# Half-size first loads with VectorE sums, and two mid weights made by an accumulating DMA, in a causal convolution kernel

## The chip, the cores and the metric

The kernel runs on one core of a Trainium2 chip (trn2). The time is device microseconds of one execution. Before the change it is 783.65 us (median of 6 runs, 783.41 to 783.91, beside the runs of the changed kernel). A profile is one further execution, seen by the hardware profiler; its span is about 2 us shorter than the time. PE is TensorE, DVE is VectorE, ACT is ScalarE, POOL is GpSimd, SP is SyncE.

All runs quoted are of one state (fast). A ratio is the mean time of one kernel's fast runs over that of the other's of the same rounds, so it isn't quite the ratio of the medians that are quoted beside it.

## The reference

```python
B, S, D, K = 8, 4096, 512, 8
for k in range(K):
    shifted = x if k == 0 else np.concatenate(
        [np.zeros((B, k, D), np.float32), x[:, :-k, :]], axis=1)
    out += np.matmul(shifted, kernel[k])
```

Eight taps, each a 512x512 matrix. The error allowed is that of bf16 inputs with f32 sums.

## The kernel before: the parts that matter

The kernel computes the taps with a three-level Karatsuba-like scheme. For that it needs sums of rows of the transposed input and differences of taps. A tap lies in `W[a, b, c]` with each index LO or HI; an index MID means a difference, so `W[MID, HI, HI] = W[HI, HI, HI] - W[LO, HI, HI]`. There are 19 such mid weights.

The input is split into 128 runs of 256 rows, one run a partition; block i holds 8 rows of each run, in two halves h. I write x00, x01, x10, x11, x20 ... for block i, half h. Each half is loaded by GpSimd (f32 to bf16 in the DMA), then transposed to `XT`. x00, x01 and x10 are transposed by PE through PSUM; from x11 on a DMA issued by SyncE does it. `H` is the history: the last rows of the neighbouring run.

```python
def load(out, src):
    nc.gpsimd.dma_start(out=out, in_=src)

def transpose_x(i, h):                       # from x11 on
    nc.sync.dma_start_transpose(out=XT[:, 4 * h:4 * h + 4, :]..., in_=xin[i, h]...)

def mid_dve(*which):                         # all 19 mid weights
    o, u, v = mid(*which)
    tt(o, u, v, SUB)

def sums_pe(name, k, *sums):                 # row sums of x00 and the history, on PE
    ...
    for n, t in enumerate(ts_):
        src, idt = (xin[0, 0][:, t], ident) if t >= 0 else (H[:, 8 + t], identh)
        nc.tensor.matmul(pw[:, h, c * P:(c + 1) * P], lhsT=src[:, c * P:(c + 1) * P],
                         rhs=idt, start=n == 0, stop=n == len(ts_) - 1, ...)

load(H[1:P, 4:8], xr[0:P - 1, RUN - 4:RUN, :])
load_x(0, 0)
# ... later, in GpSimd's order:
# load_w(4), history, load_w(6), load_w(5), load_w(7), load_x(0, 1), load_x(1, 0),
# load_w(0), load_w(2), load_w(1), load_w(3), load_x(1, 1), load_x(2, 1), load_x(2, 0)
```

Node 0 is built from 16 plain products (`direct`, 4 matmuls each); the other 95 nodes have 9 products. A node's PSUM sum often starts from a value that ScalarE writes there (`node_seed`), on which the matmuls then add.

Of the kernel before, what the change touches and what calls it, by code (L numbers as in the profile page):

```python
# [22 lines left out]
def kernel(  # L23
# [6 lines left out]
    nc = tc.nc  # L30
# [53 lines left out]
    def load_x(i, h):  # L84
        xin[i, h] = xpool.tile([P, 4, D], bf, name="xin")
        load(xin[i, h], xr[:, K * i + 4 * h:K * i + 4 * h + 4, :])
# [45 lines left out]

# [6 lines left out]
    load(H[1:P, 4:8], xr[0:P - 1, RUN - 4:RUN, :])  # L139
    load_x(0, 0)  # L140
    ident = spool.tile([P, P], bf, name="ident")
    make_identity(nc, ident)

    identh = spool.tile([P, P], bf, name="identh")
    nc.gpsimd.tensor_copy(out=identh, in_=ident)
    nc.gpsimd.memset(identh[:, 0:P:G], 0.0)
    identn = spool.tile([P, P], bf, name="identn")
    nc.gpsimd.tensor_scalar_mul(out=identn, in0=ident, scalar1=-1.0)  # L148
# [20 lines left out]

    bank = {}  # L170

    def mid_pe(h, k, *which):
        o, u, v = mid(*which)
        bank[which, h] = pair(k)
        for c in range(2):
            pw = bank[which, h][:, c]
            nc.tensor.matmul(pw, lhsT=ident, rhs=u[:, 2 * h + c], start=True, stop=False)
            nc.tensor.matmul(pw, lhsT=identn, rhs=v[:, 2 * h + c], start=False, stop=True)

    def mid_act(h, *which):  # L180
        nc.scalar.copy(out=mid(*which)[0][:, 2 * h:2 * h + 2], in_=bank[which, h])
# [13 lines left out]

    def sums_pe(name, k, *sums):

        pw = bank[name] = pair(k)
        for h, ts_ in enumerate(sums):
            for c in range(DC):  # L200
                for n, t in enumerate(ts_):
                    src, idt = (xin[0, 0][:, t], ident) if t >= 0 else (H[:, 8 + t], identh)
                    nc.tensor.matmul(pw[:, h, c * P:(c + 1) * P], lhsT=src[:, c * P:(c + 1) * P],
                                     rhs=idt, start=n == 0, stop=n == len(ts_) - 1,
                                     skip_group_check=True)
# [141 lines left out]





    load_w(4)
    transpose_pe("xh", 2, H, 5, 8)
    sums_pe("d4a", 1, (-4, 0), (-3, 1))
    load(H[1:P, 1:4], xr[0:P - 1, RUN - 7:RUN - 4, :])
    load_w(6)
    sums_pe("d4b", 2, (-2, 2), (-1, 3))
    nc.vector.tensor_copy(out=XF[:, 0:3], in_=bank["xh"])  # L358
    transpose_pe("xf", 2, xin[0, 0], 0, 4)
    load_w(5)  # L360
    nc.vector.tensor_copy(out=D4[:, 0:2], in_=bank["d4a"])
    nc.scalar.copy(out=D4[:, 2:4], in_=bank["d4b"])
    n0.p = {0: pair(0), 1: pair(1)}
    fill(pair(3))
    load_w(7)
    direct(0, 2)
    direct(0, 1)
    direct(0, 3)
    nc.scalar.copy(out=XF[:, 3:7], in_=bank["xf"])  # L369
    sums_pe("e4a", 2, (-5, -1), (-6, -2))  # L370
    nc.vector.memset(XF[:, 0:3, 0:D:G], 0.0)
    tt(D2, XF[:, 0:5], XF[:, 2:7], ADD)
    direct(2, 3)
    tt(F21, D2[:, 0:4], D2[:, 1:5], ADD)
    mid_dve(1, LO, HI)
    sums_pe("e4b", 2, (-7, -3))
    direct(1, 2)
    direct(0, 0)
    load_x(0, 1)
    tt(D1, XF[:, 2:4], XF[:, 3:5], ADD)  # L380
    mid_dve(2, LO, HI)
    nc.scalar.copy(out=E4[:, 3:1:-1], in_=bank["e4a"])
    mid_dve(2, LO, LO)
    load_x(1, 0)
    load_w(0)
    nc.vector.tensor_copy(out=E4[:, 1], in_=bank["e4b"][:, 0])
    direct(1, 3)
    direct(1, 1)
    transpose_pe("x1", 2, xin[0, 1], 0, 4)
    nc.scalar.copy(out=XT[:, 4:8], in_=bank["x1"])  # L390
# [60 lines left out]
    load_x(2, 0)
# [201 lines left out]
```

## Time and profile before

| | before |
|---|---|
| time, median | 783.65 us |
| span of the profile | 780.9 us |
| PE busy | 767.4 us, 98% |
| x01, x10, x11 landed | 25.0, 27.5, 40.1 us |
| transposing DMA of x11: issued, to landing | 40.20 us, 4.9 us |
| PE's wait behind x11 | 0.74 us, at 48 us |

Read it from the end of the chain backwards: the span is PE's work plus what PE doesn't get to do at the start. So only PE's waits before 98 us are to be had. The prediction below shows the lines.

### The profile page before, as it was taken

To read this page: it belongs to the slowest core of one execution; us is meant where nothing else is said; L and a number is where in the kernel's file an instruction comes from. 1 tells how busy PE (TensorE), PEld (TensorE's weight loads), DVE (VectorE), ACT (ScalarE), POOL (GpSimd) and SP (SyncE) were. 2 spreads that over 40 slices of the span, in tenths; PEclk is the share of its full clock that TensorE was granted. 3 is DMA by queue.
4 is the path that set the end of the run, shared out by engine and by line. 5 is a ranking of instruction groups with operands and counts; after the bars stand their busy time and mean duration, and the time that the engine had idled before them with its cause. 6 is when DMAs were issued, how large, how long until landed. Compare 5 with 4: busy or idle time off the path is not lost.

```text
span 780.9 us, 9507 instructions
## 1 busy us (share of the span) xinstructions
PE 767.4 (98%) x3620; PEld 349.0 (45%) x3620; DVE 659.3 (84%) x764; ACT 283.2 (36%) x460; POOL 42.8 (5%) x83
## 2 busy tenths in 40 slices
PE   7899999999999999999999999999999999999997
PEld 4444444444444444444444444444444444444443
DVE  4899888888888889888898888898888898888895
ACT  2453433333333333343324343333343333343332
POOL 5000000000000000000000000000000000000000
PEclk9999999999999999999999999999999999999999
DMA  9963979778788777878777788877787877788753
GB/s 163 210 120 114 237 176 207 169 187 167 178 179 206 174 176 173 177 184 194 184 171 168 179 190 188 191 166 179 165 187 187 195 170 182 166 172 200 179 153 123
DMA packets 159229, 138.37 MB, mean 177 GB/s; under 512 B 130130, under 2 KB 134226, under 8 KB 159184
## 3 DMA queue, kind: packets, MB, share of 16 engines
q1 hardware_dynamic: 145312, 98.84, 46.3%
q0 software_dynamic: 13728, 38.66, 31.1%
q8 instruction: 28, 0.46, 0.2%
q10 hardware_dynamic: 144, 0.26, 0.1%
q14 instruction: 17, 0.14, 0.1%
HBM read 77.32 MB, written 67.11 MB: 185 GB/s over the span
## 4 chain that ended last, share of the span: by engine, by line
PE 94%; DMA 3%; DVE 1%; POOL 1%; issue 0%; ACT 0%; DVEq 0%; POOLq 0%
PE pp L215 94%; DMA xin<-in_x_dram 2%; DMA XT<-xin 1%; POOL w L80 0%; DVE D L76 0%; PE pp L192 0%; DVE pp L76 0%; ACT XT L390 0%; DVE y L76 0%; POOL D L80 0%; DVEq L648 0%; POOL xin L80 0%; POOL identn L148 0%; PE pp L186 0%; POOL ident masks.py:199 0%
## 5 line engine op out<-in xcount | busy, mean ns | idle before, releaser
L215 PE MATMUL pp<-w,D 128*128 128x512 bf16 x3280 | 715.8, 379 | 1.7 <-DMA w<-in_kernel_dram 0.9
L215 PEld LDWEIGHTS <-D 128*128 128x128 bf16 x3280 | 320.2, 98 | 390.4 <-issue 2.8
L76 DVE TENSOR_TENSOR D<-D 128x2048 bf16<-128x2048 bf16 (+2 forms) x250 | 227.2, 948 | 3.4 <-ACT D L369 3.4
L76 DVE TENSOR_TENSOR y<-pp,ms 128x1024 f32<-128x1024 f32 (+1 forms) x121 | 146.4, 1212 | 45.3 <-PE pp L215 45.3
L76 DVE TENSOR_TENSOR D<-XT 128x2048 bf16<-128x2048 bf16 (+2 forms) x153 | 142.5, 947 | 12.1 <-DMA XT<-xin 10.4
L262 ACT COPY pp<-pp 128x512 f32<-128x512 f32 x95 | 54.1, 570 | 260.6 <-PE pp L215 260.6
L274 ACT COPY pp<-pp 128x512 f32<-128x512 f32 x95 | 54.2, 570 | 167.1 <-PE pp L215 165.6
L76 DVE TENSOR_TENSOR pp<-dts,pp 128x512 f32<-128x512 f32 x95 | 65.7, 691 | 43.9 <-ACT dts L280 42.6
L317 ACT COPY ms<-pp 128x1024 f32<-128x1024 f32 x60 | 61.0, 1016 | 35.0 <-PE pp L215 33.0
L80 POOL DMA_DIRECT2D xin<-in_x_dram x64 | 34.0, 531 | 692.5 <-DMA XT<-xin 675.8
L290 DVE SCALAR_TENSOR_TENSOR pp<-pp,dts 128x512 f32<-128x512 f32 x95 | 66.0, 695 | 3.2
L280 ACT COPY dts<-pp 128x512 f32<-128x512 f32 x95 | 57.5, 606 | 0.0
L276 ACT ACTIVATE pp<-pp 128x512 f32<-128x512 f32 x95 | 56.1, 590 | 0.8 <-PE pp L215 0.8
L215 PE MATMUL pp<-w,XT 128*128 128x512 bf16 x120 | 30.8, 379 | 0.0
L76 DVE TENSOR_TENSOR w<-w,w 128x2048 bf16<-128x2048 bf16 x19 | 22.9, 1219 | 1.5 <-DMA w<-in_kernel_dram 1.3
L215 PEld LDWEIGHTS <-XT 128*128 128x128 bf16 x120 | 11.7, 98 | 14.2
L186 PE MATMUL pp<-zero,ident 128*128 128x512 bf16 x20 | 6.7, 493 | 3.1 <-POOL ident masks.py:199 3.1
L215 PE MATMUL pp<-w,F 128*128 128x512 bf16 x36 | 8.7, 379 | 0.2 <-DVE pp L76 0.2
L215 PE MATMUL pp<-w,w 128*128 128x512 bf16 x36 | 8.3, 379 | 0.0
L192 PE MATMUL pp<-ident,xin 128*128 128x128 bf16 x48 | 3.2, 219 | 3.6 <-DMA xin<-in_x_dram 1.4
L80 POOL DMA_DIRECT2D w<-in_kernel_dram x8 | 6.1, 785 | 0.5 <-DMA w<-in_kernel_dram 0.5
L358 DVE COPY D<-pp 128x1536 bf16<-128x1536 bf16 x1 | 1.0, 958 | 6.1 <-PE pp L192 6.1
(59 smaller groups left out, 78.7 us busy)
## 6 DMA issues: line engine op xcount, KB each, us to landing
out_dram<-y SPq DMA_DIRECT2D x123, 512.0 KB, 3.4
xin<-in_x_dram POOLq DMA_DIRECT2D x64, 512.0 KB, 6.0
w<-in_kernel_dram POOLq DMA_DIRECT2D x8, 512.0 KB, 15.7
out_dram<-ms SPq DMA_DIRECT2D x2, 512.0 KB, 5.4
out_dram<-f SPq DMA_DIRECT2D x2, 512.0 KB, 6.3
XT<-xin SPq DMA_TRANSPOSE x61, 6.1
D<-in_x_dram POOLq DMA_DIRECT2D x1, 508.0 KB, 5.6
D<-in_x_dram POOLq DMA_DIRECT2D x1, 381.0 KB, 9.4
```

The lines of the kernel that those rows point to most:

```text
L76: nc.vector.tensor_tensor(out=o, in0=a, in1=b, op=op)
L80: nc.gpsimd.dma_start(out=out, in_=src)
L186: nc.tensor.matmul(pw[:, h], lhsT=ident, rhs=zero, start=True, stop=True)
L192: nc.tensor.transpose(o[:, t - t0, c * P:(c + 1) * P], src[:, t, c * P:(c + 1) * P], ident)
L215: nc.tensor.matmul(bank, lhsT=comp[:, c * P:(c + 1) * P], rhs=w[:, c, :], start=start and c == 0, stop=c == DC - 1, skip_group_check=True)
L262: nc.scalar.copy(out=n.q[:, 0], in_=n.q[:, 1])
L274: nc.scalar.copy(out=n.p[b_][:, 1], in_=n.q[:, 1])
L276: nc.scalar.mul(out=n.p[b_][:, 1], in_=n.q[:, 1], mul=-1.0)
L280: nc.scalar.copy(out=n.dts, in_=n.q[:, 0])
L290: nc.vector.scalar_tensor_tensor(out=p[:, 0], in0=p[:, 1], scalar=-1.0, in1=n.dts, op0=MUL, op1=SUB)
L317: nc.scalar.copy(out=ms[b_], in_=p)
L358: nc.vector.tensor_copy(out=XF[:, 0:3], in_=bank["xh"])
```

## The change

Its intent is to start node 0 earlier (first loads in halves, row sums by VectorE instead of PE) and to relieve VectorE of two mid weights (ScalarE writes the negated LO weight, a DMA adds the HI weight to it in SBUF). The order of nearly everything in the first 100 us moves too; most of that is cut here. `load_h(a, b)` loads a part of the history, `load_x(0, 0, 0, 2)` the first two rows of x00. `XF` holds transposed rows of the history and of x00, `D4` their sums.

```diff
+    load_h(-4, -2)
+    load_x(0, 0, 0, 2)
-    load(H[1:P, 4:8], xr[0:P - 1, RUN - 4:RUN, :])
-    load_x(0, 0)
...
+    def mid_neg(u, v):
+        nc.scalar.mul(out=W[MID, u, v], in_=W[LO, u, v], mul=-1.0)
+
+    def mid_acc(u, v):
+        nc.gpsimd.dma_start(out=W[MID, u, v], in_=W[HI, u, v], accum_op=ADD)
...
-    def sums_pe(name, k, *sums):
...
+    transpose_pe("x0", 2, xin[0, 0], 0, 2)
+    nc.vector.tensor_copy(out=XF[:, 4:6], in_=bank["x0"])
+    nc.vector.tensor_copy(out=XF[:, 0:2], in_=bank["h0"])
+    tt(D4[:, 0:2], XF[:, 0:2], XF[:, 4:6], ADD)
...
+    load_x(1, 1)
+    mid_acc(HI, HI)
+    mid_acc(LO, HI)
...
+    load_x(2, 0)
...
+    load_x(2, 1)
...
-    mid_dve(0, HI, HI)
...
-    mid_dve(0, LO, HI)
```

More of the change, by code (lines that the diff above doesn't have):

```diff
@@ L82, with load_x @@
     xin = {}
-    def load_x(i, h):
-        xin[i, h] = xpool.tile([P, 4, D], bf, name="xin")
-        load(xin[i, h], xr[:, K * i + 4 * h:K * i + 4 * h + 4, :])
+    def load_x(i, h, a=0, b=4):
+        if a == 0:
+            xin[i, h] = xpool.tile([P, 4, D], bf, name="xin")
+        t0 = K * i + 4 * h
+        load(xin[i, h][:, a:b], xr[:, t0 + a:t0 + b, :])
     def transpose_x(i, h):
@@ L138, with load_h @@
     H = D421
-    load(H[1:P, 4:8], xr[0:P - 1, RUN - 4:RUN, :])
-    load_x(0, 0)
+    def load_h(a, b):
+        load(H[1:P, 8 + a:8 + b], xr[0:P - 1, RUN + a:RUN + b, :])
+    load_h(-4, -2)
+    load_x(0, 0, 0, 2)
     ident = spool.tile([P, P], bf, name="ident")
     make_identity(nc, ident)
-    identh = spool.tile([P, P], bf, name="identh")
-    nc.gpsimd.tensor_copy(out=identh, in_=ident)
-    nc.gpsimd.memset(identh[:, 0:P:G], 0.0)
-    identn = spool.tile([P, P], bf, name="identn")
-    nc.gpsimd.tensor_scalar_mul(out=identn, in0=ident, scalar1=-1.0)
     zero = spool.tile([P, D], bf, name="zero")
@@ L168, in mid_dve @@
         tt(o, u, v, SUB)
+    def mid_neg(u, v):
+        nc.scalar.mul(out=W[MID, u, v], in_=W[LO, u, v], mul=-1.0)
+    def mid_acc(u, v):
+        nc.gpsimd.dma_start(out=W[MID, u, v], in_=W[HI, u, v], accum_op=ADD)
     bank = {}
-    def mid_pe(h, k, *which):
-        o, u, v = mid(*which)
-        bank[which, h] = pair(k)
-        for c in range(2):
-            pw = bank[which, h][:, c]
-            nc.tensor.matmul(pw, lhsT=ident, rhs=u[:, 2 * h + c], start=True, stop=False)
-            nc.tensor.matmul(pw, lhsT=identn, rhs=v[:, 2 * h + c], start=False, stop=True)
-    def mid_act(h, *which):
-        nc.scalar.copy(out=mid(*which)[0][:, 2 * h:2 * h + 2], in_=bank[which, h])
     def fill(pw):
@@ L194, in transpose_pe @@
         bank[name] = o[:, 0:t1 - t0]
-    def sums_pe(name, k, *sums):
-        pw = bank[name] = pair(k)
-        for h, ts_ in enumerate(sums):
-            for c in range(DC):
-                for n, t in enumerate(ts_):
-                    src, idt = (xin[0, 0][:, t], ident) if t >= 0 else (H[:, 8 + t], identh)
-                    nc.tensor.matmul(pw[:, h, c * P:(c + 1) * P], lhsT=src[:, c * P:(c + 1) * P],
-                                     rhs=idt, start=n == 0, stop=n == len(ts_) - 1,
-                                     skip_group_check=True)
     for r in range(2):
@@ L346, with first_run @@
     C0, C1 = W[MID, HI, MID], W[MID, LO, MID]
-    load_w(4)
-    transpose_pe("xh", 2, H, 5, 8)
-    sums_pe("d4a", 1, (-4, 0), (-3, 1))
-    load(H[1:P, 1:4], xr[0:P - 1, RUN - 7:RUN - 4, :])
+    def first_run(z):
+        nc.vector.memset(z[:, :, 0:D:G], 0.0)
+    transpose_pe("h0", 0, H, 4, 6)
+    load_h(-2, 0)
+    load_x(0, 0, 2, 4)
+    load_w(4)
+    transpose_pe("x0", 2, xin[0, 0], 0, 2)
+    nc.vector.tensor_copy(out=XF[:, 4:6], in_=bank["x0"])
+    nc.vector.tensor_copy(out=XF[:, 0:2], in_=bank["h0"])
@@ L356 @@
+    first_run(XF[:, 0:2])
+    tt(D4[:, 0:2], XF[:, 0:2], XF[:, 4:6], ADD)
+    transpose_pe("xb", 2, xin[0, 0], 2, 4)
+    n0.p = {0: pair(0), 1: pair(1)}
+    transpose_pe("h1", 0, H, 6, 8)
+    nc.scalar.copy(out=XF[:, 6:8], in_=bank["xb"])
+    nc.scalar.copy(out=XF[:, 2:4], in_=bank["h1"])
+    direct(0, 0)
+    load_h(-7, -4)
+    first_run(XF[:, 2:4])
     load_w(6)
-    sums_pe("d4b", 2, (-2, 2), (-1, 3))
-    nc.vector.tensor_copy(out=XF[:, 0:3], in_=bank["xh"])
-    transpose_pe("xf", 2, xin[0, 0], 0, 4)
+    transpose_pe("he", 2, H, 1, 4)
@@ L360 @@
     load_w(5)
-    nc.vector.tensor_copy(out=D4[:, 0:2], in_=bank["d4a"])
-    nc.scalar.copy(out=D4[:, 2:4], in_=bank["d4b"])
-    n0.p = {0: pair(0), 1: pair(1)}
+    tt(D4[:, 2:4], XF[:, 2:4], XF[:, 6:8], ADD)
+    direct(0, 3)
+    direct(0, 1)
+    nc.scalar.copy(out=F0, in_=XF[:, 4])
     fill(pair(3))
-    load_w(7)
-    direct(0, 2)
-    direct(0, 1)
-    direct(0, 3)
-    nc.scalar.copy(out=XF[:, 3:7], in_=bank["xf"])
-    sums_pe("e4a", 2, (-5, -1), (-6, -2))
-    nc.vector.memset(XF[:, 0:3, 0:D:G], 0.0)
@@ L372 @@
-    tt(D2, XF[:, 0:5], XF[:, 2:7], ADD)
-    direct(2, 3)
-    tt(F21, D2[:, 0:4], D2[:, 1:5], ADD)
-    mid_dve(1, LO, HI)
-    sums_pe("e4b", 2, (-7, -3))
-    direct(1, 2)
-    direct(0, 0)
-    load_x(0, 1)
-    tt(D1, XF[:, 2:4], XF[:, 3:5], ADD)
-    mid_dve(2, LO, HI)
-    nc.scalar.copy(out=E4[:, 3:1:-1], in_=bank["e4a"])
-    mid_dve(2, LO, LO)
-    load_x(1, 0)
-    load_w(0)
-    nc.vector.tensor_copy(out=E4[:, 1], in_=bank["e4b"][:, 0])
-    direct(1, 3)
-    direct(1, 1)
-    transpose_pe("x1", 2, xin[0, 1], 0, 4)
@@ L390 @@
-    nc.scalar.copy(out=XT[:, 4:8], in_=bank["x1"])
-    load_w(2)
-    mid_dve(1, LO, LO)
-    direct(1, 0)
-    transpose_pe("x2", 2, xin[1, 0], 0, 4)
-    mid_dve(2, LO, MID)
-    load_w(1)
-    tt(D4[:, 4:8], XF[:, 3:7], XT[:, 4:8], ADD)
-    direct(2, 1)
-    nc.vector.tensor_copy(out=XT[:, 2:4], in_=bank["x2"][:, 2:4])
+    direct(0, 2)
+    direct(2, 2)
+    tt(E4[:, 1:4], bank["he"], XF[:, 1:4], ADD)
+    first_run(E4[:, 1:4])
+    tt(D2, XF[:, 1:6], XF[:, 3:8], ADD)
+    load_w(7)
+    direct(1, 0)
@@ new lines @@
+    direct(1, 3)
+    load_x(0, 1)
+    tt(D1, XF[:, 3:5], XF[:, 4:6], ADD)
+    direct(1, 2)
+    mid_dve(1, LO, HI)
+    load_x(1, 0)
+    direct(1, 1)
+    mid_dve(2, LO, HI)
+    tt(F21, D2[:, 0:4], D2[:, 1:5], ADD)
+    load_w(0)
+    mid_dve(1, LO, LO)
+    mid_dve(2, LO, LO)
+    direct(2, 3)
+    mid_dve(2, LO, MID)
+    mid_neg(HI, HI)
+    mid_neg(LO, HI)
+    transpose_pe("x1", 2, xin[0, 1], 0, 4)
+    nc.vector.tensor_copy(out=XT[:, 4:8], in_=bank["x1"])
+    tt(D4[:, 4:8], XF[:, 4:8], XT[:, 4:8], ADD)
@@ L400 @@
+    direct(2, 0)
+    nc.scalar.copy(out=C0[:, 0:2], in_=XT[:, 6:8])
+    prep_d41(HI)
+    transpose_pe("x2", 2, xin[1, 0], 0, 4)
+    nc.scalar.copy(out=XT[:, 2:4], in_=bank["x2"][:, 2:4])
+    load_w(2)
+    direct(3, 0)
     prep_d42(HI)
     nc.scalar.copy(out=XT[:, 0:2], in_=bank["x2"][:, 0:2])
-    nc.scalar.copy(out=C0[:, 0:2], in_=XT[:, 6:8])
+    direct(3, 3)
     tt(T4, XT[:, 4:8], XT[:, 0:4], ADD)
     direct(3, 1)
-    prep_d41(HI)
-    tt(T42[:, 0:2], D4[:, 6:8], T4[:, 0:2], ADD)
@@ L407 @@
-    direct(3, 0)
-    nc.scalar.copy(out=C1, in_=XT[:, 0:4])
-    direct(2, 0)
-    nc.scalar.copy(out=F0, in_=XF[:, 3])
-    direct(3, 3)
-    fill(pair(2))
-    tt(D41[:, 1], T4[:, 0], T4[:, 1], ADD)
-    load_w(3)
-    tt(T42[:, 2:4], T4[:, 0:2], T4[:, 2:4], ADD)
-    node_a1(1)
-    direct(2, 2)
+    fill(pair(2))
+    load_w(3)
+    nc.scalar.copy(out=C1, in_=XT[:, 0:4])
+    direct(3, 2)
+    tt(D41[:, 1], T4[:, 0], T4[:, 1], ADD)
+    node_a1(1)
+    tt(D41[:, 0], D4[:, 7], T4[:, 0], ADD)
@@ L418 @@
+    direct(2, 1)
+    load_w(1)
+    node_a0(nodes[1])
+    tt(T42[:, 0:2], D4[:, 6:8], T4[:, 0:2], ADD)
+    tt(T42[:, 2:4], T4[:, 0:2], T4[:, 2:4], ADD)
+    node_u(nodes[1])
+    load_x(1, 1)
+    mid_acc(HI, HI)
+    mid_acc(LO, HI)
+    tt(D421[:, 0], D42[:, 7], T42[:, 0], ADD)
     node_e(nodes[0], 0)
-    tt(D41[:, 0], D4[:, 7], T4[:, 0], ADD)
-    node_a0(nodes[1])
-    node_u(nodes[1])
-    direct(3, 2)
+    node_seed(nodes[1], 0)
     mid_dve(1, HI, HI)
-    node_seed(nodes[1], 0)
     prep_d27()
+    node_v(nodes[1], 0)
@@ L426 @@
+    mid_dve(2, HI, LO)
+    tt(D421[:, 1:4], T42[:, 0:3], T42[:, 1:4], ADD)
+    node_seed(nodes[1], 1)
     node_dts(nodes[1])
-    node_seed(nodes[1], 1)
     tt(D42[:, 3], D4[:, 1], D4[:, 3], ADD)
-    node_v(nodes[1], 0)
-    tt(D421[:, 0], D42[:, 7], T42[:, 0], ADD)
-    load_x(1, 1)
-    node_v(nodes[1], 1)
-    tt(D421[:, 1:4], T42[:, 0:3], T42[:, 1:4], ADD)
-    node_a1(2)
-    mid_dve(2, HI, LO)
-    transpose_x(1, 1)
-    mid_dve(1, HI, LO)
-    node_d(nodes[1], 0)
-    node_l(nodes[1], 0, LO)
@@ L440 @@
-    mid_dve(2, HI, MID)
-    nc.scalar.copy(out=D4[:, 2:4], in_=T4[:, 2:4])
-    node_d(nodes[1], 1)
-    load_x(2, 1)
-    node_e(nodes[0], 1)
-    node_u(nodes[2])
-    node_l(nodes[1], 0, HI)
-    node_e(nodes[1], 0)
-    node_a0(nodes[2])
-    node_seed(nodes[2], 0)
-    prep_d421(HI)
-    load_x(2, 0)
-    mid_dve(2, HI, HI)
-    node_l(nodes[1], 1, LO)
-    node_l(nodes[1], 1, HI)
-    nc.scalar.copy(out=U1, in_=XT[:, 0])
+    load_x(2, 0)
+    node_d(nodes[1], 0)
+    mid_dve(1, HI, LO)
@@ new lines @@
+    mid_dve(2, HI, HI)
+    node_a1(2)
+    node_l(nodes[1], 0, HI)
+    node_v(nodes[1], 1)
+    load_x(2, 1)
+    node_d(nodes[1], 1)
+    mid_dve(2, HI, MID)
+    prep_d421(HI)
+    node_l(nodes[1], 0, LO)
+    node_a0(nodes[2])
+    node_l(nodes[1], 1, HI)
+    node_e(nodes[1], 0)
+    node_e(nodes[0], 1)
+    nc.scalar.copy(out=D4[:, 2:4], in_=T4[:, 2:4])
+    node_u(nodes[2])
+    node_seed(nodes[2], 0)
+    node_seed(nodes[2], 1)
+    node_l(nodes[1], 1, LO)
+    node_dts(nodes[2])
+    transpose_x(1, 1)
@@ L456 @@
+    nc.scalar.copy(out=D42[:, 3], in_=T42[:, 3])
     node_v(nodes[2], 0)
+    node_v(nodes[2], 1)
     prep_d4(HI)
-    nc.scalar.copy(out=D42[:, 3], in_=T42[:, 3])
-    node_seed(nodes[2], 1)
-    node_v(nodes[2], 1)
-    node_dts(nodes[2])
-    mid_dve(0, HI, HI)
-    node_e(nodes[1], 1)
     prep_d41(HI)
     node_d(nodes[2], 0)
-    node_l(nodes[2], 0, HI)
-    tt(A1[:, 0], C0[:, 1], C1[:, 0], ADD)
-    prep_d42(HI)
-    node_d(nodes[2], 1)
-    transpose_x(2, 0)
-    mid_dve(0, LO, HI)
     node_a1(3)
@@ L473 @@
     node_l(nodes[2], 0, LO)
+    mid_dve(0, LO, LO)
+    mid_dve(0, HI, LO)
+    prep_d42(HI)
+    node_l(nodes[2], 0, HI)
     node_a0(nodes[3])
+    node_d(nodes[2], 1)
+    node_u(nodes[3])
     node_e(nodes[2], 0)
-    mid_dve(0, LO, LO)
+    node_e(nodes[1], 1)
+    node_seed(nodes[3], 0)
     tt(D421[:, 0:4], D42[:, 3:7], D42[:, 4:8], ADD)
-    node_u(nodes[3])
     node_l(nodes[2], 1, HI)
     node_seed(nodes[3], 1)
-    node_seed(nodes[3], 0)
+    tt(A1[:, 0], C0[:, 1], C1[:, 0], ADD)
     node_dts(nodes[3])
+    node_v(nodes[3], 0)
@@ L483 @@
+    node_v(nodes[3], 1)
     mid_dve(1, MID, HI)
-    node_v(nodes[3], 1)
+    node_l(nodes[2], 1, LO)
     node_d(nodes[3], 1)
-    mid_dve(0, HI, LO)
-    node_v(nodes[3], 0)
+    node_e(nodes[2], 1)
     node_d(nodes[3], 0)
-    node_l(nodes[2], 1, LO)
+    mid_dve(1, MID, LO)
     node_a1(4)
-    mid_dve(1, MID, LO)
-    tt(D21[:, 2:4], C1[:, 0:2], C1[:, 2:4], ADD)
     node_l(nodes[3], 1, HI)
     node_l(nodes[3], 0, LO)
+    nc.scalar.copy(out=U1, in_=XT[:, 0])
+    node_a0(nodes[4])
+    tt(D21[:, 2:4], C1[:, 0:2], C1[:, 2:4], ADD)
@@ L495 @@
     mid_dve(2, MID, MID)
-    node_e(nodes[2], 1)
-    load_x(3, 0)
-    node_l(nodes[3], 0, HI)
-    node_a0(nodes[4])
-    tt(D21[:, 0:2], C0[:, 0:2], C1[:, 0:2], ADD)
-    node_u(nodes[4])
-    node_e(nodes[3], 0)
-    node_l(nodes[3], 1, LO)
-    tt(A1[:, 1], C1[:, 0], C1[:, 1], ADD)
+    node_dts(nodes[4])
+    tt(D21[:, 0:2], C0[:, 0:2], C1[:, 0:2], ADD)
+    node_l(nodes[3], 0, HI)
+    node_e(nodes[3], 0)
+    node_u(nodes[4])
+    tt(A1[:, 1], C1[:, 0], C1[:, 1], ADD)
+    node_l(nodes[3], 1, LO)
@@ L505 @@
+    load_x(3, 0)
+    transpose_x(2, 0)
     mid_dve(2, MID, LO)
+    node_seed(nodes[4], 0)
+    node_seed(nodes[4], 1)
+    node_v(nodes[4], 0)
     mid_dve(2, MID, HI)
-    node_seed(nodes[4], 0)
-    node_v(nodes[4], 0)
-    node_seed(nodes[4], 1)
-    node_dts(nodes[4])
+    node_a1(5)
     node_d(nodes[4], 0)
-    node_a1(5)
     node_v(nodes[4], 1)
+    node_l(nodes[4], 0, HI)
     prep_m()
-    node_l(nodes[4], 0, HI)
     node_l(nodes[4], 0, LO)
+    node_e(nodes[3], 1)
+    node_u(nodes[5])
@@ L517 @@
+    node_d(nodes[4], 1)
     node_a0(nodes[5])
-    node_e(nodes[3], 1)
-    node_d(nodes[4], 1)
-    node_u(nodes[5])
+    node_y(nodes[4], 0, LO)
+    node_y(nodes[4], 0, HI)
+    prep_d4(LO)
+    node_l(nodes[4], 1, HI)
+    tt(F21[:, 1], D21[:, 0], D21[:, 1], ADD)
+    node_dts(nodes[5])
+    tt(F21[:, 0], D2[:, 0], D21[:, 0], ADD)
     node_seed(nodes[5], 0)
     node_l(nodes[4], 1, LO)
-    tt(F21[:, 0], D2[:, 0], D21[:, 0], ADD)
-    node_l(nodes[4], 1, HI)
-    node_y(nodes[4], 0, LO)
-    node_y(nodes[4], 0, HI)
+    node_v(nodes[5], 0)
@@ L527 @@
+    node_y(nodes[4], 1, LO)
     store(0, LO, 0, first[0, LO, 0])
-    tt(F21[:, 1], D21[:, 0], D21[:, 1], ADD)
-    node_dts(nodes[5])
-    node_v(nodes[5], 0)
+    store(0, HI, 0, first[0, HI, 0])
+    node_d(nodes[5], 0)
     prep_d27()
     node_seed(nodes[5], 1)
-    store(0, HI, 0, first[0, HI, 0])
-    load_x(3, 1)
-    node_y(nodes[4], 1, LO)
     node_v(nodes[5], 1)
-    node_d(nodes[5], 0)
+    node_a1(6)
     node_d(nodes[5], 1)
+    transpose_x(2, 1)
+    node_y(nodes[4], 1, HI)
+    store(0, HI, 1, first[0, HI, 1])
@@ L539 @@
+    node_l(nodes[5], 0, HI)
+    node_l(nodes[5], 0, LO)
     tt(F21[:, 2:4], D21[:, 1:3], D21[:, 2:4], ADD)
-    node_l(nodes[5], 0, LO)
-    node_l(nodes[5], 0, HI)
-    node_a1(6)
-    node_l(nodes[5], 1, HI)
+    node_y(nodes[5], 0, HI)
     node_u(nodes[6])
-    prep_d4(LO)
-    store(0, LO, 1, first[0, LO, 1])
-    node_y(nodes[4], 1, HI)
-    node_a0(nodes[6])
     node_y(nodes[5], 0, LO)
     prep_d41(LO)
-    transpose_x(2, 1)
+    node_l(nodes[5], 1, HI)
     node_l(nodes[5], 1, LO)
-    store(0, HI, 1, first[0, HI, 1])
+    store(0, LO, 1, first[0, LO, 1])
@@ L554 @@
     node_seed(nodes[6], 0)
+    node_a0(nodes[6])
     node_v(nodes[6], 0)
-    node_y(nodes[5], 0, HI)
     tt(D21[:, 0:2], D2[:, 0:2], D2[:, 1:3], ADD)
-    node_dts(nodes[6])
+    store(1, LO, 0, first[1, LO, 0])
     node_seed(nodes[6], 1)
     node_v(nodes[6], 1)
+    node_dts(nodes[6])
+    prep_d42(LO)
+    node_d(nodes[6], 0)
+    store(1, HI, 0, first[1, HI, 0])
+    node_y(nodes[5], 1, HI)
+    node_a1(7)
+    load_x(3, 1)
+    node_y(nodes[5], 1, LO)
+    store(1, HI, 1, first[1, HI, 1])
@@ L561 @@
+    store(1, LO, 1, first[1, LO, 1])
     tt(D21[:, 2:4], D2[:, 2:4], D2[:, 3:5], ADD)
-    node_d(nodes[6], 0)
-    prep_d42(LO)
-    node_y(nodes[5], 1, HI)
     node_d(nodes[6], 1)
-    store(1, LO, 0, first[1, LO, 0])
-    node_y(nodes[5], 1, LO)
-    store(1, HI, 0, first[1, HI, 0])
-    node_a1(7)
-    store(1, HI, 1, first[1, HI, 1])
     prep_d4(HI)
-    store(1, LO, 1, first[1, LO, 1])
     for k, (i, a) in enumerate(order):
```

## The prediction

> **What bounds the kernel now.** I read the page first (engine shares and slices), then the table by stretches, then the chain of waits, then the timeline of the first 60 us.
>
> ```profile
> PE 767.4 (98%) x3620; PEld 349.0 (45%) x3620; DVE 659.3 (84%) x764; ACT 283.2 (36%) x460; POOL 42.8 (5%) x83
> PE   7899999999999999999999999999999999999997
> ```
>
> TensorE (PE) has work for 98% of a 780.9 us span; only the first slices and the last are not full. The stretches (length, then PE, weight loads, VectorE, ScalarE, GpSimd busy, granted clock, DMA share, GB/s) show where the rest is:
>
> ```profile
> 10.00:25.00 15.00, 11.44 (x98) 6.75 (x95) 9.73 (x11) 3.89 (x3) 3.54 (x5) 1.00 1.18 206
> 25.00:33.80 8.80, 7.63 (x58) 4.24 (x58) 7.49 (x10) 5.72 (x5) 1.08 (x2) 1.00 1.20 203
> 33.80:48.80 15.00, 14.26 (x66) 6.18 (x66) 14.48 (x19) 10.40 (x16) 0.53 (x1) 1.00 0.93 161
> 98.00:776.40 678.40, 678.34 (x3142) 306.74 (x3140) 577.03 (x668) 242.56 (x405) 29.07 (x55) 1.00 0.77 178
> ```
>
> From 98 us PE is idle for 0.06 us in 678. The work there is the same products before and after, so nothing can be won there. The program has 95 nodes of 36 product matmuls and one of 64, so 3484; from 33.8 us on they go at 0.216 us each (741.6 us of PE time for the 3428 left there), so a product (4 matmuls) is 0.865 us. All products together are 753 us; 28 of the 781 us are start, waits and tail. The tail (4.6 us after 776.4) is untouched. In the head, the DMA share is full from 10 to 33.8 us, so arrivals set the pace there. The chain of waits (start, length, what) agrees:
>
> ```profile
> 7.61 17.42 DMA xin<-in_x_dram
> 25.08 1.08 PE pp L192 x16
> 26.18 1.87 ACT XT L390
> 28.10 1.05 PE pp L192 x16
> ...
> 33.90 13.30 PE pp L215 x60
> ...
> 47.45 0.69 DVE D L76
> 48.13 0.62 DVE pp L76
> 48.79 21.96 PE pp L215 x100
> ```
>
> The second input block lands at 25.0 us, PE transposes it, ScalarE takes 1.87 us to empty the PSUM bank, only then can the third block (it landed at 27.5: issued 13.84, 13.6 us to landing) be transposed in the same bank. After that PE is solid until 47.9, where a VectorE chain behind the transposed fourth block (x11) costs 0.74 us.
>
> **What the Trainium skill says.** "Perfetto Trace Analysis", section DMA Optimizations: splitting DMAs lets some work start sooner if the DMA engines are generally idle. Here they are not: the share is full, so only the first piece comes earlier, not the last byte. "VectorE: DVE Perf Modes", the perf-mode tier table: a 2048-element bf16 add takes 1224 ns; the trace has 1219 for the 19 mid weights. "Collectives: The Full Stack", the bandwidth ceiling section: a DMA add needs two source reads. No run so far shows one. "DMA: Bandwidth & Descriptors", SWDGE vs HWDGE vs iDMA: an accumulate can only be issued from GpSimd, and inside a DMA engine queues of both kinds are served in turns, so the adds slow a transposing DMA that runs beside them. The trace agrees: the transposing DMA issued at 50.8 us, alone, landed in 4.3 us; the one at 40.2, beside one input load, in 4.9; the one at 85.9, beside two stores, in 7.7.
>
> **Part 1: half loads, VectorE sums.** Bytes are the same, so I keep the landings read off issue times plus times to landing: first full input block 9.4 us, tap-4 weight 12.5, third piece of history 14.2, tap 6 at 16.8, tap 5 at 20.05, tap 7 at 22.6, x01 25.0, x10 27.5. GpSimd loses three identity-making instructions (0.29 + 0.13 + 0.54 us) and gains two more issues (about 0.55 each), so weight 4 is issued no later. PE loses 56 small sum matmuls (16 + 16 + 16 + 8) at a spacing of 0.055 us, 3.1 us, and gains 16 transposes (44 instead of 28 before x01), 0.9 us. VectorE makes the sums: two copies from PSUM (0.68 each, as the row of the x2 copy), a memset (0.14), an add of 1024 elements (0.69): ready at about 9.3 + 2.3 = 11.6 us, before weight 4 at 12.5. So the first product starts at 12.5 rather than 13.8.
>
> What counts is how many of the 16 first products ("direct") stand before 25.0. Before: 8. Changed: the first at 12.5 to 13.4; history transposes at 14.2 to 14.9; three with tap 4 and a 0.43 us filler to 17.9; one with tap 6 to 18.8; then wait for tap 5 at 20.05; five of them to 24.4. So 10 instead of 8, and PE then waits 0.6 us for x01. **Gain 2 x 0.865 = 1.7 us.** Next, x01's bank is emptied by VectorE (about 1.3 us, scaled from 0.958 for 1536 elements) rather than ScalarE (1.87): the x10 transposes start at 27.6, when the block is there, instead of 28.1. **Gain 0.5.** At 28.5 us the change is 2.2 us ahead.
>
> **Part 2: reordered work up to 48 us.** In the old order one direct product stands between node 1's middle product and its first seeded one, while ScalarE writes the seed. In the new order there is none: PE drain (0.16) + seed (0.57) + two handovers (0.1) is about 0.8 us. **Loss 0.8.** Then PE has 19 products, transposes and a filler from 27.6: 16.4 + 1.3 + 0.3 + 0.8, so it has done node 2's last seeded product at 46.4; before it was 47.9. Next it needs sums of x11. That block lands at 40.1 (issued 26.45, 13.7 to landing) in both, since the same bytes are ahead of it in the queue, and its transposing DMA ends at 45.1. VectorE needs 1.14 us (start to start, 45.17 to 46.31) and 0.69 for two sums, so PE goes on at 47.05 at the earliest. Before it went on at 48.79. **Gain up to here 1.7, if the transposing DMA is as quick.** Two mid weights now stand before the second difference of node 2, which comes at 46.31 + 0.6 + 0.6 + 1.15 + 1.15 + 1.15 + 0.69 = 51.65, while PE arrives at 47.05 + 5 x 0.865 = 51.4: about 0.35 lost. **1.35 left.**
>
> **Part 3: two mid weights by copy and DMA.** VectorE loses two adds of 1.22 us (2.4 us) in a stretch where it is 97% to 100% busy. ScalarE gets two negated copies of 1.9 us each (the row of the 2048-element copy), at 17 to 21 us, where it waits 7.7 us anyway: free. The DMAs read the bytes of an ordinary load (two bf16 sources for one f32), so my estimate is 2.6 us each, the cadence of the weight landings, or up to 5. They queue behind x11, so they run from 40.1 to about 45 to 50. Their results are wanted by the level-1 difference at about 53.5 us: in time. But they run beside x11's transposing DMA, which had 2.6 us of load beside it before and now has 5 us or more: 6 us to landing instead of 4.9 is my choice between 4.9 and 7.7, so **1.1 lost**, as VectorE and PE both stand behind it. The small stall at 72.66 (0.19 us) may go, and PE is solid afterwards.
>
> Sum: 2.2 - 0.8 = 1.4 ahead at 46; the wait for x11 sums turns that to 1.7 - 1.1 against the old stall, minus 0.35 and plus 0.19: about 0.4 us. Since the old stall's other part (VectorE busy with two mid weights) goes for good, I lean a little to the good side: gain 0.7, so **782.8 us**.
>
> **Rivals.** (a) The gain of the first 28 us survives whole, plus the two stalls of 0.74 and 0.19: 783.5 - 3.1 = 780.4. For it: VectorE is the releaser at 48.13. Against: x11 still lands at 40.1. (b) The accumulating DMAs are much slower than a load, say 8 us each: x11's transposing takes 7.7 or more and the weights come at 56 instead of 53.5: 786 or so. For it: no row of this trace has such a DMA. Against: deadlines have 4 us of slack at 5 us each. (c) The transposing DMA of the first half of row block 2 is issued later, behind a ScalarE copy at about 58 us, and land at 62 to 64 where VectorE wants them at 63: a new stall of up to 1 us: 784. (d) It is hidden entirely, as the head is bound by arrivals up to 40.1: 783.5.
>
> **Range and chances.** For faster by 2% the change would have to take 15.7 us of the 28 that are not products, while the start up to the first transpose (8.4) and the tail (4.6) alone are 13: next to impossible. Slower by 2% needs a stall of 16 us from slow adds: barely possible. Rival (a) sets the low end, 780.6, with a little less than its whole; (b) and (c) set the high one, 785.0. Faster 0.01, same 0.97, slower 0.02.
>
> **What would show each step.** First product at 12.5 us, 10 direct products before the transposes at 25.0, the second at 27.6; PE idle 0.8 before node 1's first seeded product near 36 us; VectorE waiting longer than 0.52 us for the transposed x11; that DMA at 6 us to landing; accumulates at 2.6 to 5 us apart. The prediction is wrong if the transposing DMA is not slowed, if accumulates are far slower than loads, or if PE idles after 60 us.

## The result

The changed kernel takes 789.18 us (median of 6, 788.79 to 790.01) against 783.65: ratio 1.0071, 95% interval 1.0058 to 1.0084. That is clearly slower, by 5.5 us, though within 2%. The predicted range, 780.6 to 785.0, doesn't hold it.

The chain of waits of the changed kernel (start, length, what) answers to that shown of before:

```profile
7.59 18.52 DMA xin<-in_x_dram
26.15 1.08 PE pp L187 x16
27.52 13.53 DMA xin<-in_x_dram
41.14 9.48 DMA XT<-xin
50.71 1.24 DVE D L76
52.04 0.70 DVE D L76
52.79 7.57 PE pp L199 x24
```

Before, the chain ran along PE from 28.1 to 47 us. Now it runs along x11: its load to 41.1, its transposing DMA (`XT<-xin`) for 9.5 us, two VectorE sums, and only then PE. The timeline has the two waits in brackets at the end of a line. Before:

```profile
45.17 1.23 DVE L76 TENSOR_TENSOR D<-XT 128x2048 bf16<-128x2048 bf16 x1 [0.52 <-DMA XT<-xin]
48.79 12.28 PE L215 MATMUL pp<-w,D 128*128 128x512 bf16 x56 [0.74 <-DVE pp L76]
```

After:

```profile
31.57 0.90 POOL L174 DMA_DIRECT2D w<-w  x1 [3.52 <-ACT XT L399]
34.05 0.86 POOL L174 DMA_DIRECT2D w<-w  x1 [1.58 <-DMA w<-in_kernel_dram]
34.60 0.88 POOL L80 DMA_DIRECT2D xin<-in_x_dram  x1
50.71 1.23 DVE L76 TENSOR_TENSOR D<-XT 128x2048 bf16<-128x2048 bf16 x1 [6.03 <-DMA XT<-xin]
52.79 14.66 PE L199 MATMUL pp<-w,D 128*128 128x512 bf16 x55 [5.10 <-DVE D L76]
```

PE waits 5.10 us where it waited 0.74. The three POOL lines are the two adds and x20, issued long before x11 had landed. The DMA view gives 12.0, 12.0 and 14.1 us from issue to landing, so the adds landed at 43.6 and 46.05 and x20 at 48.7, one after the other behind x11 (41.0).

The last column but two of the stretches is the granted clock. After:

```profile
48.00:50.00 2.00, 0.00 (x0) 0.00 (x0) 0.00 (x0) 0.00 (x0) 0.00 (x0) 1.00 1.03 194
50.00:52.00 2.00, 0.00 (x0) 0.00 (x0) 1.23 (x1) 0.00 (x0) 0.55 (x1) 0.62 0.00 0
52.00:54.00 2.00, 1.21 (x3) 0.43 (x4) 1.96 (x3) 0.00 (x0) 0.00 (x0) 0.50 0.75 111
54.00:56.00 2.00, 2.00 (x6) 0.76 (x5) 2.00 (x3) 0.57 (x1) 0.00 (x0) 0.50 0.76 152
58.00:60.00 2.00, 2.00 (x11) 0.90 (x10) 1.95 (x3) 1.97 (x3) 0.00 (x0) 1.00 0.00 0
```

After the idle stretch PE works at half clock from 50.5 to 57.3 us: 6 matmuls in 2 us instead of 11. The same trace has an earlier half-clock stretch, 12.95 to 16.36 us, after 3.4 us in which PE had been busy for 1.07 us. It will have cost nothing at the end, since PE waited 1.35 us for x01 afterwards. The kernel before has none.

To see where the time goes I use a mark that both kernels have: ScalarE's first copy of each node k, right after that node's first product (the rows of the timeline with the form 128x512 f32 that follow PE).

| node k | before, us | after, us | difference |
|---|---|---|---|
| 1 | 34.88 | 34.40 | -0.5 |
| 2 | 41.07 | 39.73 | -1.3 |
| 3 | 50.77 | 54.77 | +4.0 |
| 4 | 57.71 | 64.10 | +6.4 |
| 9 | 97.29 | 103.20 | +5.9 |

The two orders differ, so not every mark stands after the same work: counted in the two programs, mark 1 comes one product later in the changed kernel, marks 2 and 3 one product (0.87 us) earlier; 4 and 9 agree. In equal work the head leads by 1.35 us at mark 1 and by 0.5 at mark 2. When PE stops for x11 it has done the same 30 products in both, at 48.05 us before and 47.69 after: a lead of 0.36 us. By mark 4 that has become a loss of 6.4 us, and the loss doesn't grow after that: the two profiled spans differ by 6.4 us too (780.9 and 787.3), the medians of all runs by 5.5.

### The profile page after: what moved, and what is told of

It is laid out like the page before. It is cut to its first block, busy times and chain, and to the rows that moved or that the text cites. A ratio compares the mean times of both kernels' runs of the same rounds, so it can differ in the third digit from the quotient of the medians.

```text
span 787.3 us, 9363 instructions
## 1 busy us (share of the span) xinstructions
PE 764.4 (97%) x3509; PEld 347.9 (44%) x3580; DVE 658.7 (84%) x766; ACT 284.3 (36%) x461; POOL 44.8 (6%) x84
## 4 chain that ended last, share of the span: by engine, by line
PE 90%; DMA 6%; DVE 1%; POOL 1%; issue 1%; ACT 0%; DVEq 0%; SPq 0%; ACTq 0%; POOLq 0%
PE pp L199 90%; DMA xin<-in_x_dram 4%; DMA XT<-xin 2%; DVE D L76 1%; DVE y L76 0%; POOL w L80 0%; ACT pp L258 0%; POOL D L80 0%; POOL xin L80 0%; PE pp L187 0%; DVE pp L76 0%; DVEq L642 0%; SPq L284 0%; POOL ident masks.py:199 0%; DVE pp L274 0%
## 5 line engine op out<-in xcount | busy, mean ns | idle before, releaser
L76 DVE TENSOR_TENSOR D<-D 128x1024 bf16<-128x1024 bf16 x252 | 228.5, 947 | 0.4 <-DMA w<-in_kernel_dram 0.2
L76 DVE TENSOR_TENSOR pp<-dts,pp 128x512 f32<-128x512 f32 x95 | 65.6, 691 | 43.8 <-ACT dts L264 42.2
L76 DVE TENSOR_TENSOR w<-w,w 128x2048 bf16<-128x2048 bf16 x17 | 20.2, 1218 | 0.0
L297 ACT COPY y<-pp 128x1024 f32<-128x1024 f32 x4 | 4.1, 1016 | 4.6 <-PE pp L199 4.6
```

The source lines that it names most:

```text
L76: nc.vector.tensor_tensor(out=o, in0=a, in1=b, op=op)
L297: nc.scalar.copy(out=y, in_=p)
```

## The experiments

Two theories. **Q**: the transposing DMA of x11 can't finish before GpSimd's queue has run dry, so every transfer queued behind x11 delays it. **R**: the half loads and the new order cost the time. A third, **A**, is a variant of Q: the add itself is what holds the transposing DMA up.

### e1: the two weights back on VectorE

```diff
-    mid_neg(HI, HI)
-    mid_neg(LO, HI)
...
-    mid_acc(HI, HI)
-    mid_acc(LO, HI)
...
+    mid_dve(0, HI, HI)
+    mid_dve(0, LO, HI)
     mid_dve(1, MID, HI)
```

> The changed kernel without the negated copies and the accumulating DMAs: the two weights are VectorE subtractions again, everything else stays. Theory Q (the transposing DMA of x11 lands about 1.9 us after the last transfer queued ahead of it by GpSimd): only one input load is left ahead of it, so it lands in 4.6 to 5 us instead of 9.5, PE's stall of 5.1 us shrinks below 1.5, its clock stays at 1.00, and the time is 782.5 to 784.5. Rival R (the half loads and the new order cost the time): it stays above 787.

Measured: 785.47 us (783.9 to 786.72, 4 runs), ratio 1.0024. x11's transposing DMA took 5.3 us and PE's wait behind it 0.44 us. The mechanism is as Q says; R as the whole cause falls. But the time is above the 784.5 that I had set, and PE has a new wait:

```profile
57.88 4.49 PE L199 MATMUL pp<-w,D 128*128 128x512 bf16 x20 [1.38 <-DVE w L76]
```

VectorE, with the two weights again, is late with the level-1 difference (`mid_dve(1, MID, HI)`, which is made from these two). So with both at that place in the new order, they cost PE a wait. (The clock was at 0.50 from 12.6 to 19.5 us in this profile, and at 1.00 from there on; x01's transposes started 0.15 us later than in the changed kernel.)

### e2: plain loads in place of the adds

```diff
-    mid_acc(HI, HI)
-    mid_acc(LO, HI)
+    load(W[MID, HI, HI], kr[:, :, 0, :])
+    load(W[MID, LO, HI], kr[:, :, 2, :])
```

> The changed kernel with each accumulating DMA replaced by a plain weight load of the same size into the same tile (wrong result on purpose). Theory Q: the bytes in the queue count, not the add: x11's transposing DMA takes 9.5 us again and the time is 788.5 to 790. Rival A (the add, or SBUF as its source, is what holds the transposing DMA up): it lands in 5 to 6 us and the time is 783 to 785.

Measured: 790.88 us (790.08 to 791.75), ratio 1.0095. Its output is wrong, which doesn't matter for the time. The transposing DMA took 9.5 us, just as with the adds, and VectorE waited for it longer than in the changed kernel:

```profile
51.48 1.23 DVE L76 TENSOR_TENSOR D<-XT 128x2048 bf16<-128x2048 bf16 x1 [6.16 <-DMA XT<-xin]
```

So A falls: two transfers of that size in that place do the harm, added or not. (The time is 0.9 us over the range that I gave; x01 landed 0.5 us later in this run.)

### e3: the adds after x11 is transposed

```diff
-    mid_acc(HI, HI)
-    mid_acc(LO, HI)
...
-    load_x(2, 1)
...
     transpose_x(1, 1)
+    gate = spool.tile([P, 1], bf, name="gate")
+    nc.gpsimd.tensor_copy(out=gate, in_=XT[:, 4, 0:1])
+    mid_acc(HI, HI)
+    mid_acc(LO, HI)
+    load_x(2, 1)
```

> The changed kernel with the two accumulating DMAs issued only after x11 has been transposed (GpSimd reads one column of the result first). Theory Q: the transposing DMA has one input load ahead of it and lands in 4.6 to 5 us; the adds land at 50 to 53 us, just before they are wanted; the time is 782.5 to 784.5. Rival R: above 787. If the adds come too late for the level-1 difference, PE stalls 1 to 2 us near 55 us instead: 785.

Measured: 783.30 us (783.0 to 784.49), ratio 1.0003, result right. The transposing DMA took 5.1 us. PE's waits behind x11 and for the late adds are about half a microsecond each:

```profile
48.19 8.22 PE L199 MATMUL pp<-w,D 128*128 128x512 bf16 x35 [0.48 <-DVE D L76]
...
56.95 4.49 PE L199 MATMUL pp<-w,D 128*128 128x512 bf16 x20 [0.53 <-DVE w L76]
```

The adds landed at 52.0 and 55.6 us, the second later than the 53 I had expected, and VectorE waited 1.46 us for it. With the two adds moved behind x11's transposing DMA, all of the loss is gone. (x21's load moves with them; in the changed kernel it waited for x11's transposition anyway, until 51.17 us.) Against e1 (same first loads, x11 as quick) it is 2.2 us better in the medians, but e1's runs spread by 2.8 us, I had put both of its weights at one place in VectorE's order, and the intervals of the two ratios overlap. So it suggests, and doesn't show, that taking the weights from VectorE is worth something, if the DMAs don't stand in front of x11.

### e6: x20 held back, the adds in place

```diff
-    load_x(2, 0)
...
-    load_x(2, 1)
...
     transpose_x(1, 1)
+    gate = spool.tile([P, 1], bf, name="gate")
+    nc.gpsimd.tensor_copy(out=gate, in_=XT[:, 4, 0:1])
+    load_x(2, 0)
+    load_x(2, 1)
```

> The changed kernel with the adds where they are, but the input load x20 held back until x11 has been transposed. Theory Q: two adds of 2.5 us are ahead of the transposing DMA instead of three transfers, so it lands in about 6.9 us instead of 9.5; PE's stall falls from 5.1 to about 2.5 us and is too short for the clock to drop; time 784 to 785.5. Rival (only the adds count, not what is behind them): 9.5 us and 789 stay.

Measured: 784.78 us (783.58 to 785.75), ratio 1.0017. The DMA view of the transposing DMA, and PE's wait:

```profile
DMA to landing us min/median/max: 6.9/6.9/6.9
```

```profile
50.23 2.12 PE L199 MATMUL pp<-w,D 128*128 128x512 bf16 x9 [2.50 <-DVE D L76]
```

6.9 and 2.5 us, both as Q had said. After this wait the clock stayed at 1.00. The rule can now be read over the kernels up to e7, the next experiment:

| kernel | last transfer queued when x11 landed | it landed | transposing DMA landed | later by |
|---|---|---|---|---|
| before | x21 | 43.15 | 45.1 | 2.0 |
| changed | x20, behind two adds | 48.7 | 50.6 | 1.9 |
| e1 | x20 | 43.8 | 46.1 | 2.3 |
| e2 | x20, behind two loads | 49.6 | 51.3 | 1.7 |
| e3 | x20 | 43.8 | 46.05 | 2.2 |
| e6 | second add | 46.2 | 48.1 | 1.9 |
| e7 | x21, behind two adds | 48.35 | 50.2 | 1.8 |

(Each landing is issue time plus time to landing.) The kernel before obeyed it already, with one load in the queue.

What goes on in between can be seen in part. The DMA view of a window counts the packets that started in it, by queue. In the changed kernel:

| window, us | GpSimd's queue | transposing DMA |
|---|---|---|
| 41.2 to 45.0 | 226 | 0 |
| 45.5 to 46.5 | 49 | 49 |
| 46.5 to 48.2 | 39 | 577 |
| 48.2 to 50.7 | 1 | 1448 |

The transposing DMA has 2080 small packets (0.52 MB, 250 bytes each), GpSimd's transfers have few large ones (0.80 MB in those 226, 3.5 KB each). In the second window as many of each went, 49 and 49, as turns by packet would give. At that rate few of the 2080 get through while GpSimd's queue lasts, and most follow when it is dry. Why none at all started before 45.3 us, 4.2 us after the issue (1.3 us in the kernel before, 2.7 in e6), stays open.

### e7: the kernel before, with this one part of the change

```diff
+    mid_neg(HI, HI)
+    mid_neg(LO, HI)
     transpose_pe("x1", 2, xin[0, 1], 0, 4)
...
     load_x(1, 1)
+    mid_acc(HI, HI)
+    mid_acc(LO, HI)
...
-    mid_dve(0, HI, HI)
...
-    mid_dve(0, LO, HI)
```

> The kernel before with this one part of the change: two mid weights made by negated copies and accumulating DMAs queued behind x11. Theory Q: two adds and x21 are ahead of x11's transposing DMA, so it lands in about 9.5 us instead of 4.9; PE's wait near 48 us grows from 0.7 to about 5 us, the clock drops, and the time is 788 to 790. Rival R (order and half loads are to blame): 783 to 784.5.

Measured: 788.75 us (788.37 to 789.54), ratio 1.0070. The transposing DMA took 10.0 us, and PE's wait is back:

```profile
53.00 7.28 PE L221 MATMUL pp<-w,D 128*128 128x512 bf16 x26 [4.98 <-DVE pp L76]
```

The half-clock stretch behind it was shorter, 3.4 us. So the two weights by copy and add make the whole loss, without the half loads and the new order; and as e3 keeps the two copies without loss, it is the adds' place in the queue.

### e4 and e4b: PE kept busy in its wait

The Trainium skill's page "TensorE: Matmul & The Clock Gate", Part 1, says that the array goes to half rate after an idle window of about 3.4 us. In the changed kernel the clock falls 2.8 us after PE's last matmul, in e7 4.6 us after it; in e6, with a wait of 2.5 us, it doesn't. To price it, dummy matmuls go into the wait (11 pairs in e4, 7 in e4b).

```diff
+    for _ in range(11):        # e4b: range(7)
+        fill(pair(3))
     node_a1(3)
```

> The changed kernel with 22 dummy matmuls (4.75 us) in PE's wait for x11. The wait itself stays and x11's transposing DMA still takes 9.5 us. If the granted clock of 0.50 from 51 to 57 us costs what it seems to (24 matmuls in 7.6 us instead of 5.2), the clock stays 1.00 and the time falls by 2.0 to 2.5 us to about 786.9. Rival: the cold clock is hidden behind VectorE, which is behind as well: less than 0.7 us.

> As the run with 22 dummy matmuls, but with 14, since 22 took 7.1 us (0.32 each) and held node 3's first product up by 2.3 us past the end of the wait. 14 take 4.5 us and end inside the wait. If the cold clock costs what it seems to, node 3's first product starts with its operands near 53 us, the clock is 1.00 and the time falls by 1.5 to 2.5 us to about 787. Rival: it is hidden, less than 0.7 us.

e4 measured 788.96 us (788.25 to 789.17), ratio 1.0068: no gain, and inconclusive. The 22 matmuls took 7.1 us, 0.32 us each, and held node 3 up for 2.3 us after its operands were there. e4b measured 787.71 us (787.24 to 787.98), ratio 1.0054, with the clock at 1.00 after the wait and PE's timeline so:

```profile
47.48 4.49 PE L181 MATMUL pp<-zero,ident 128*128 128x512 bf16 x14
52.74 12.54 PE L199 MATMUL pp<-w,D 128*128 128x512 bf16 x56 [0.77 <-DVE D L76]
```

56 matmuls take 12.5 us, where 55 took 14.7 in the changed kernel. Node 4's mark comes at 61.92 us instead of 64.10, so the cold clock costs 2.2 us there. At the end the median is 1.5 us lower (in ratios, 1.0071 to 1.0054, 1.3 us), but the intervals of the two ratios overlap, so what reaches the end is rough.

### e5: the first loads whole

```diff
+    load_h(-4, 0)
+    load_x(0, 0)
-    load_h(-4, -2)
-    load_x(0, 0, 0, 2)
...
-    load_h(-2, 0)
-    load_x(0, 0, 2, 4)
```

> The changed kernel with the first history and input block loaded whole, not in halves. If the halves themselves delay everything queued behind them by about 1 us, x00 is complete at 9.4 instead of 10.75 us, x01 lands near 25.0 instead of 26.1, x11 near 40.2 instead of 41.1, and the time is 0.8 to 1.2 us less, about 788.2; the 9.5 us of the transposing DMA and PE's stall of 5 us stay. Rival: the landings do not move, or the stall swallows them: 789.2.

Measured: 788.56 us (788.07 to 790.02), ratio 1.0069. x01's transposes started at 25.75 us rather than 26.15, so 0.4 and not 1 us came back, and the end time isn't told apart from the changed kernel's. The transposing DMA still took 9.4 us and PE still waited 5.1 us. Why x01 comes at 25.7 and not at 25.0, as in the kernel before, is left open.

### e8: whole loads, and the adds after x11

This joins the edits of e5 and e3.

> Whole first loads and the adds issued after x11 is transposed: both known costs of the change are taken out, the VectorE sums and the new order stay. The run with only the adds moved gave 783.3, the whole loads took 0.6 us off the changed kernel, so 782.7, which would be 0.6 us under the kernel before. Rival: PE waits for the adds near 57 us as long as it gains: 783.5.

Measured: 782.58 us (782.19 to 783.77, 5 runs) against 783.62, ratio 0.9993, interval 0.9979 to 1.0006: the median is where it was expected, but the interval includes 1. By the marks it leads the kernel before at node 3 by 2.5 us (48.31 against 50.77; 1.6 in equal work, as the mark stands one product earlier), at node 9 by 1.2 us (96.04 against 97.29), at node 10 by 1.5 (103.81 against 105.30), at node 11 by 0.8 (112.25 against 113.07). So what the head wins is given back in part by node 9 and again between 104 and 112 us. I didn't follow that up.

### e10, e11, e12 and e13: x11 transposed by PE

If nobody waits for a transposing DMA behind the adds, they should do no harm where they are. x11 goes through a PSUM bank as x01 and x10 do (e10: changed kernel; e11, e12, e13: with whole loads too). A few neighbouring copies and sums move as well.

```diff
+    transpose_pe("x3", 1, xin[1, 1], 0, 4)
...
+    nc.scalar.copy(out=XT[:, 4:8], in_=bank["x3"])     # e12, e13
...
-    transpose_x(1, 1)
```

> The changed kernel, adds and loads in their places, with x11 transposed on PE (16 matmuls, 0.9 us) and copied by ScalarE and VectorE, so that nobody waits for a transposing DMA behind the adds. Theory Q: the adds themselves harm nobody else; PE's stall of 5.1 us at 47.7 goes to below 0.5, and the time is 782.5 to 784 (6 us less, plus 0.9 for the transposes). Rival: the adds also delay something later (mid weights, x20), and the time stays above 785.

> As the run with x11 transposed on PE, with whole first loads too. With x01 landing 0.4 us earlier and PE solid from there on, 0.4 us less than that run: 782.2 to 783.6. Rival: no gain of the whole loads, as in a kernel whose stall swallows it.

e10 measured 784.98 us (784.69 to 785.05) and e11 784.14 (783.98 to 784.41), both with a wrong result that I hadn't meant, so their times prove little. In both, PE's wait of 5.1 us was gone; the longest after 40 us was 1.5 us, for ScalarE.

> The two runs with x11 transposed on PE gave a wrong result by an ordering mistake of mine (one ScalarE copy overwrote a sum before it was read) and waited 1.5 us on ScalarE. Mended: the copy of D4 moved to where ScalarE idles, the earlier sum back in its place, one ScalarE copy of the whole transposed block; whole first loads; the adds stay where the change has them. Expected: correct, no PE wait over 0.7 us after 40 us although the adds are in the queue, node 3's first product at about 48 us, and 782 to 783 us. Rival: the adds still hold up mid weights or x20: 784.5 or more.

e12 measured 781.74 us (781.34 to 782.51), ratio 0.9981, and was wrong still. The Trainium skill's page "PSUM — Partial Sum Buffer", The four PSUM rules, has a likely reason: a PE transpose clears the bank's written bits, and a matmul without the first flag then overwrites instead of adding. Node 2's sum would then have lost its seed. The kernel has a dummy pair after its other transposes. Against e12, e13 changes this:

> The run before it was still wrong: after the PE transposes nothing set the bank up again for a sum that starts from a ScalarE seed, which the other two transposed blocks have a dummy pair of matmuls for. With such a pair (0.43 to 0.6 us on PE) and node 2's two halves swapped so that PE doesn't wait for it: correct, no PE wait over 0.7 us after 30 us with the adds in the queue behind x11, and 782.0 to 782.6, below the 783.6 of the kernel before. If adds held anything else up in a kernel with right data, 784 or more.

```diff
+    fill(pair(1))
+    node_seed(nodes[2], 1)
     node_seed(nodes[2], 0)
-    node_seed(nodes[2], 1)
...
+    node_v(nodes[2], 1)
     node_v(nodes[2], 0)
-    node_v(nodes[2], 1)
```

e13 measured 783.03 us (782.76 to 784.33), ratio 0.9997 (0.9984 to 1.0011), and its result is right, which fits the page. PE's waits after 40 us, in its timeline:

```profile
45.57 0.59 PE L181 MATMUL pp<-zero,ident 128*128 128x512 bf16 x2 [0.23 <-ACT XT L446]
46.00 7.22 PE L199 MATMUL pp<-w,D 128*128 128x512 bf16 x32
53.61 6.63 PE L199 MATMUL pp<-w,D 128*128 128x512 bf16 x30 [0.39 <-DVE pp L274]
```

The adds stand in the queue as in the changed kernel, no wait is over 0.4 us, and the time is 6.15 us below it (the whole first loads are in that too). It missed the 782.6 that I had hoped for. No version with a right result is faster than the kernel before, clear of noise.

## Why the prediction was wrong

**What bounds the kernel** held: from mark 4 on the loss didn't grow, and after 65 us PE had no wait over 0.2 us.

**Part 1** was right in its effect and off in its times. Ten of the 16 first products stood before x01, as worked out (their matmuls run from 13.5 to 24.8 us, then PE waits 1.35 us). But the landings weren't kept: x00 was complete at 10.75 us instead of 9.4, weight 4 at 13.4 instead of 12.5, x01 at 26.1 instead of 25.0, x11 at 41.0 instead of 40.1. The first product started at 13.5, not 12.5; the profile names ScalarE's copy of a transposed bank as its releaser. e5 tells the two apart: there weight 4 was in at 12.5, and the first product still waited for that copy, until 13.98. My sum had no such copies. x10's transposes started at 28.5, not 27.6. The quicker bank was had (2.4 us from x01's transposes to x10's, 3.0 before), but x01's lateness took more: two products less 0.43 us, so 1.3 us ahead at 28.5 and not 2.2.

**Part 2** was right in its loss and, through Part 1, wrong in its end. PE waited 0.66 us (0.8 predicted) before node 1's first seeded product. But PE was done with node 2's last seeded product at 47.69 us, not 46.4, so 0.36 us ahead of the kernel before and not 1.5. The 1.3 us of Part 1 less 0.66 would leave 0.64; where the other 0.3 us went I don't know.

**Part 3** is where it failed, at this step: "6 us to landing instead of 4.9 is my choice between 4.9 and 7.7, so 1.1 lost". The adds themselves were judged well: they landed 2.5 us apart (2.6 predicted), in time for the mid weights, and ScalarE's copies (1.92 us each, at 13.8 and 17.8 us) were free. But the transposing DMA took 9.5 us. I had read the 4.9 us of the kernel before as a small slowdown by one load, from the Trainium skill's sentence that both kinds of queue are served in turns ("DMA: Bandwidth & Descriptors", SWDGE vs HWDGE vs iDMA). The runs show another sum: it lands 1.7 to 2.3 us after the last transfer queued on GpSimd by then. With that rule the kernel before already told the answer: x21 landed at 43.15, the transposed x11 at 45.1. Two adds of 2.5 us and x20 in the queue make 41.0 + 7.7 + 1.9 = 50.6, which is what was measured. I had also left x20 out of the count.

**The second missing term** is the clock: none of my steps asked what a wait of 5 us does to PE. It costs 2.2 us at node 4 (e4b).

The sum in the runs' terms: the wait grows from 0.74 to 5.10 (+4.4), the cold clock (+2.2), the head's lead at the wait (-0.4), together +6.2 of the 6.4 us by which the two profiles differ, at node 4 and in their spans. The medians differ by 5.5.

**What was to show it wrong.** The prediction named three signs: the transposing DMA not slowed, adds far slower than loads, PE idle after 60 us. None came true. It failed in a direction for which it had set no sign: the transposing DMA slowed far more than by its choice.

**The rivals.** (b) had the right object and the wrong reason: it made the adds slow, "8 us each"; they were as quick as loads, and the transposing DMA waited for three quick transfers. Its 786 was the nearest of the four. (a), (c) and (d) fell: no lead survives x11, and no PE wait over 0.2 us follows after 65 us.

## What to carry to other kernels

Before putting a new transfer on a queue, look at what will wait for a DMA that is issued while the new one is still queued: the cost isn't the transfer's own 2.5 us but its delay of that DMA, and here it counted although the new data were in no hurry. Two points on one line (4.3 us alone, 4.9 beside a load) don't tell a small slowdown from "ends 2 us after the queue is dry"; check the landing times against each other before choosing a number. And price a long wait of PE twice, once for itself and once for the clock that follows.

## What the Trainium skill lacked or had wrong

- "DMA: Bandwidth & Descriptors", SWDGE vs HWDGE vs iDMA, says that inside a DMA engine the queues of both kinds are served in turns. The packet counts fit that in part (49 and 49 in one us), but a transposing DMA issued by SyncE, with its 2080 small packets, gained little by it: it landed 1.7 to 2.3 us after the last transfer in GpSimd's queue in all seven kernels of the table, in 4.9 to 10.0 us, against 4.3 us alone. The section doesn't draw this consequence. Why the first packet came up to 4.2 us after the issue no run here shows.
- No page that I read gives a duration for an accumulating DMA from SBUF to SBUF. In the changed kernel one of 512 KB (bf16) landed 2.5 us behind its predecessor, as a load of the same size with a cast did; in e3, with nothing queued ahead, the first took 4.7 us to landing and the second came 3.6 us behind it. "Collectives: The Full Stack" with its two source reads led to the right estimate.
- "Perfetto Trace Analysis", DMA Optimizations, says that splitting may let some of the work start sooner, and the whole be done sooner if the DMA engines are generally idle. It doesn't name the cost if they aren't: the first half of the history landed at 5.85 us where the whole had landed at 6.8, but the complete x00 at 10.75 instead of 9.4.
- "TensorE: Matmul & The Clock Gate", Part 1, with its idle window of about 3.4 us, agrees with the long waits: one of 5.1 us brought the granted clock to 0.50 for almost 7 us, one of 2.5 us didn't. But the window needn't be empty: in the changed kernel's head PE was busy for 1.07 us of the 3.4 us before the clock fell, in e6's for 1.50 us.
